# Moving small elementwise work from GpSimd to VectorE and ScalarE, and rotating the dense products over more PSUM banks, in a hybrid diffusion layer

## The chip, the cores and the metric

One core of a Trainium2 chip runs one program with five engines: TensorE (PE in the views, its weight loads PEld), VectorE (DVE), ScalarE (ACT), GpSimd (POOL) and SyncE (SP, which here only issues loads). The metric is device time in microseconds (us) from the program's start to its end, the median of a few executions. The profile is of one further execution.

## The reference, cut to what matters

The layer takes 512 latent tokens and 256 context tokens of width 1024. One wide input projection feeds three parallel branches and their output gates; the branches are merged, projected, and followed by a convolutional feed-forward part.

```
px, pc = split(hx @ w_in), split(hc @ w_in)          # latent, context
# branch a, HGRN2, 4 heads, forward and backward
f = sigmoid-based decay(px[1], lb);  k = (1 - lb) * sigmoid(-px[1])
a = rmsnorm(scan(q, f, k, v), g) * silu(px[4])       # per head, 128 channels
# branch b: grouped attention, 8 heads of 64, keys from context and latent
# branch c, Hyena: u = v * x1; y = irfft(rfft(u) * rfft(kern)) + u * bias; c = y * x0
m = sigmoid(g_a)*(a @ w_oa) + sigmoid(g_b)*(b @ w_ob) + sigmoid(g_c)*(c @ w_oc)
x = x + gate * rmsnorm(m @ w_out)
x = x + gate * rmsnorm((silu(conv(h @ w_up)_1) * conv(h @ w_up)_2) @ w_down)
```

## The kernel before, in words

Activations lie with channels on the partitions and tokens along the free axis. Each float32 operand of a dense product is split into a high and a low part (`split`: ScalarE copies the high part, L204, VectorE subtracts, L207), and a product takes three TensorE passes (`passes`), so that a dense product of 1024 by 128 weights against 512 tokens is 24 matmuls of 512 columns into one PSUM bank.

`Mixer.run` builds a list of such dense jobs: for each head of branch a two gate jobs and one value job, then keys, queries, Hyena inputs, then the merge, the output projection and the feed-forward. `stream` runs the list and loads and splits the weights one job ahead. Beside it run generators for the work that follows from the jobs: `hg_mixes`, `hg_states` and `hg_outputs` for branch a, `hyena` for branch c, `at_prepare`, `all_scores` and `attention` for branch b, and `second` for the norm between the halves. `weave` interleaves them by a planned time: each `yield` of a number is the delay after which a generator's next piece may be emitted. TensorE's order is pinned to that order of emission. The other engines' orders are laid by the framework's scheduler when the program is compiled: it lets a later instruction go ahead where an earlier one is planned to wait. Each engine's queue then runs in the order that was laid.

PSUM has eight banks of 512 float32 columns. `dbank` hands out the banks of `dbanks` in turn to the dense products; `cbank` hands out those of `cbanks` to everything else. Between the first stage and the attention these are two banks and six. A dense product may start when its bank has been read out: by ScalarE and VectorE in `hg_gate` (L638, L639), `conv3` (L888 to L890) or at the merge (L1277, L1292, L1294). The attention sets `dbanks` to [1, 5] while its scores take banks 2 to 4, and at its end to [0, 1]. The first product of the output projection uses bank 0 by name.

The places where GpSimd works before:
- `rstd_` (four calls, one per head of branch a): VectorE adds the epsilon (L872), GpSimd takes the power -0.5 (L873) and then builds four diagonal matrices of 128 by 128 by scaling the identity (L876); TensorE multiplies ones by them to spread the result over the partitions. In the first stage `shares` does the same with the diagonals in one VectorE operation (L470).
- `hg_gate` (16 calls, 8 of 512 columns and 8 of 256): k is the sigmoid times a per-channel factor (L642).
- `hy_spectrum` (two calls): for each of two blocks of frequencies and two signs the complex product of the spectra, of which one of the six operations is on GpSimd (L969) and five on VectorE (L968, L970 to L973); and, once per call, the product for row 0, six operations on one partition (L952 to L957).
- The power of `at_prepare` (L1152) and the load of the transform tables (L340) stay in GpSimd's queue.

Of the kernel before, what the change touches and what calls it, by code (L numbers as in the profile page):

```python
# [15 lines left out]
AF = mybir.ActivationFunctionType  # L16
ALU = mybir.AluOpType
PSUM = bass.MemoryType.PSUM
MUL, ADD, SUB = ALU.mult, ALU.add, ALU.subtract
# [11 lines left out]
C_ID, C_ONE, C_KVB, C_Q2, C_OV, C_WK, C_NWK, C_WKS, C_EPS, C_NH, NCONST = (  # L31
    0, 128, 384, 512, 516, 518, 520, 522, 524, 525, 557)
# [127 lines left out]
class Mixer:  # L160
# [335 lines left out]
    def begin(self):  # L496

        nc, i, v = self.nc, self.i, self.nc.vector
# [98 lines left out]
            pass  # L597
        self.free(cb, m, rows[1], self.slots)
        self.slots = []
        self.dbanks, self.cbanks = [0, 1], [2, 3, 4, 5, 6, 7]  # L600

    def ada_rest(self):

# [28 lines left out]
    def hg_gate(self, ps, n, col, f, k):  # L632

        nc, v = self.nc, self.nc.vector
        s, t = self.A(n), self.A(n)
        s_, t_ = s[:, :n], t[:, :n]
        lo, om = self.lb[:, 16 + col:17 + col], self.lb[:, 24 + col:25 + col]
        nc.scalar.activation(s_, ps, AF.Sigmoid)  # L638
        nc.scalar.activation(t_, ps, AF.Sigmoid, scale=-1.0)  # L639
        v.scalar_tensor_tensor(f, s_, math.exp(30.0), t_, op0=MUL, op1=ALU.min)  # L640
        v.scalar_tensor_tensor(f, f, lo, s_, op0=MUL, op1=ADD)
        nc.gpsimd.tensor_scalar(k, t_, om, 1.0, op0=MUL, op1=MUL)  # L642
        self.free(s, t)

    def group(self, col):
# [217 lines left out]
    def rstd_(self, sqs, ones_col, scale=1.0, n=T, engine=None):  # L863

        nc, v = self.nc, self.nc.vector
        nc_ = n // 128
        ps = self.cbank()
        for j, sq in enumerate(sqs):
            for c in range(nc_):
                self.mm(ps[:, 2 * c:2 * c + 2], sq[:, c * 128:(c + 1) * 128], self.cv(ones_col, 2), j == 0 and c == 0, j == len(sqs) - 1 and c == nc_ - 1)  # L870
        ms = self.A(16)
        v.tensor_scalar(ms[:, 0:nc_], ps.v(0, [(2, nc_)]), scale, EPS, op0=MUL, op1=ADD)  # L872
        nc.gpsimd.tensor_tensor(ms[:, 4:4 + nc_], ms[:, 0:nc_], self.cv(C_NH, nc_), op=ALU.pow)  # L873
        dg = self.A(n)
        for c in range(nc_):
            (engine or nc.gpsimd).tensor_scalar(dg[:, c * 128:(c + 1) * 128], self.cv(C_ID, 128), ms[:, 4 + c:5 + c], 1.0, op0=MUL, op1=MUL)  # L876
        yield 3.5
        rb = self.cbank()
        for c in range(nc_):
            self.mm(rb[:, c * 128:(c + 1) * 128], self.cv(C_ONE, 128), dg[:, c * 128:(c + 1) * 128], True, True)  # L880
        self.free(ms, dg)
        return rb
# [27 lines left out]
    def hy_spectrum(self, ch):  # L910


        nc, v, g = self.nc, self.nc.vector, self.nc.gpsimd
        uT, bufs, Y, K = [], [], {}, self.K
        cs = slice(ch * 256, ch * 256 + 256)
        for par in range(2):
            ps = self.cbank()
            for mc in range(2):
                for ct in range(2):
                    o = (2 * mc + ct) * 128  # L920
                    self.transpose(ps[:, o:o + 128], self.us[2 * ch + ct].v(2 * 128 * mc + par, [(2, 128)]))
            hh, ll = self.R(512), self.R(512)
            self.split(hh.r, ll.r, ps[:])
            uT += [(hh.r[:, mc * 256:mc * 256 + 256], ll.r[:, mc * 256:mc * 256 + 256]) for mc in range(2)]
            bufs += [hh, ll]
        yield 2.5
        for kc in range(2):
            S, y, ks = {}, {}, slice(kc * 256, kc * 256 + 256)
            for half, n in enumerate("cs"):
                ps = self.cbank()  # L930
                pe, po = ps[:, 0:256], ps[:, 256:512]
                self.dft(pe, uT, 2 * half, 0, kc)
                self.dft(po, uT, 2 * half + 1, 1, kc)
                p, e = S[n + "p"], S[n + "m"] = self.A(256), self.A(256)
                nc.scalar.activation(e[:], pe, AF.Copy)
                v.tensor_tensor(p[:], po, e[:], op=ADD)
                if kc == 0:
                    if half == 0:
                        ur = self.A(512)
                    else:  # L940
                        nc.scalar.activation(ur[0:1, :], ps[0:1, :], AF.Copy)
                if half == 0:
                    v.scalar_tensor_tensor(e[:], po, -1.0, e[:], op0=MUL, op1=ADD)
                else:
                    v.tensor_tensor(e[:], po, e[:], op=SUB)
                yield 0.3
            if kc == 0:
                row, t = self.A(512), self.A(256)
                r = row[0:1, :]
                c0, s0 = ur[0:1, 0:256], ur[0:1, 256:512]  # L950
                kc0, ks0 = self.Krow[0:1, cs], self.Krow[0:1, 512 + ch * 256:768 + ch * 256]
                g.tensor_tensor(r[:, 0:256], c0, kc0, op=MUL)  # L952
                g.tensor_tensor(r[:, 256:], c0, ks0, op=MUL)
                g.tensor_tensor(t[0:1, :], s0, ks0, op=MUL)
                g.tensor_tensor(r[:, 0:256], r[:, 0:256], t[0:1, :], op=SUB)
                g.tensor_tensor(t[0:1, :], s0, kc0, op=MUL)
                g.tensor_tensor(r[:, 256:], r[:, 256:], t[0:1, :], op=ADD)  # L957
                self.free(t, ur)
                if ch == 1:
                    self.free(self.Krow)  # L960
            else:
                self.free(bufs)
                if ch == 1:
                    self.free(self.fwd)
            for x in "pm":
                C, Sn, Kc, Ks = S["c" + x], S["s" + x], K["c" + x][ch][:, ks], K["s" + x][ch][:, ks]
                a, b, t = self.A(256), self.A(256), self.A(256)
                v.tensor_tensor(a[:], C[:], Kc, op=MUL)  # L968
                g.tensor_tensor(t[:], Sn[:], Ks, op=MUL)  # L969
                v.tensor_tensor(b[:], C[:], Ks, op=MUL)  # L970
                v.tensor_tensor(a[:], a[:], t[:], op=SUB)
                v.tensor_tensor(t[:], Sn[:], Kc, op=MUL)
                v.tensor_tensor(b[:], b[:], t[:], op=ADD)  # L973
                self.free(t, C, Sn)
                y["c" + x], y["s" + x] = a, b
                yield 2.2
            for n, (a, b, op) in enumerate((("cp", "cm", ADD), ("cp", "cm", SUB), ("sp", "sm", SUB), ("sp", "sm", ADD))):
                t, hl = self.A(256), self.R(512)
                v.tensor_tensor(t[:], y[a][:], y[b][:], op=op)
                if kc == 0 and n >= 2:  # L980
                    v.tensor_copy(t[0:1, :], r[:, (n - 2) * 256:(n - 1) * 256])
                self.split(hl.r[:, 0:256], hl.r[:, 256:512], t[:])
                Y[n, kc] = hl
                self.free(t)
                yield 0.9
            self.free(*y.values())
            if kc == 0:
                self.free(row)
        self.free([k[ch] for k in K.values()])
        return Y  # L990
# [221 lines left out]
    def attention(self):  # L1212
        nc, v = self.nc, self.nc.vector
# [26 lines left out]
        for n in range(16):  # L1240
            yield lambda: n in self.pr
            p, ready = self.pr.pop(n)
            for g in range(3):
                yield max(AT_SPLIT, ready - self.time)
                pt = Buf(self.bank((6, 0)[(n + g) % 2]))
                for j in range(2):
                    for e in range(2):
                        o = (2 * j + e) * 128
                        k = (2 * g + j + 2 * e) % 6 * 128
# [10 lines left out]
        while todo:  # L1260
            yield AT_SPLIT
            values()
        self.dbanks = [0, 1]
        self.free(self.qs, *self.ks[0], *self.ks[1], self.vhl_bufs, self.rq)


# [469 lines left out]
```

## Time and profile before

| what | value |
|---|---|
| median of 3 runs | 1106.04 us (1105.34 to 1109.14) |
| the profiled execution, its own time | 1114.44 us |
| its span, first to last instruction | 1112.7 us |
| mean granted TensorE clock | 0.989 of full speed |
| TensorE busy | 1073.2 us, 96% of the span |
| VectorE busy | 759.3 us, 68% |
| ScalarE busy | 483.3 us, 43% |
| GpSimd busy | 109.4 us, 10% |

Busy time of TensorE counts a matmul from its start to a modelled end, and successive matmuls overlap, so the idle time that is left over is time in which TensorE really had nothing to run. In the timeline rows the first number is the start in us, the second the length of the stretch, and the bracket says how long the engine was idle just before and which engine and line ended that.

### The profile page before, as it was taken

The numbers are of one execution on the slowest core, as the hardware profiler recorded it, in microseconds if no ns is written. First come the engines' busy times: TensorE is split into PE (matmuls) and PEld (weight loads), VectorE is DVE, ScalarE is ACT, GpSimd is POOL, SyncE is SP. The second block draws the span as 40 slices with busy tenths as digits, with TensorE's granted clock in tenths as the row PEclk, the third lists the DMA queues.
The fourth block names the chain that finished last, engine by engine and source line by source line (L and its number), as shares of the span: only waits on it lengthen the run. The fifth ranks groups of instructions, "written<-read, shape, count | busy, mean of one in ns | idle before, by whom it ended". The sixth has DMA issues, their size and how long they took to land.

```text
span 1112.7 us, 14365 instructions
## 1 busy us (share of the span) xinstructions
PE 1073.2 (96%) x5540; PEld 905.2 (81%) x5540; DVE 759.3 (68%) x1262; ACT 483.3 (43%) x751; POOL 109.4 (10%) x130
## 2 busy tenths in 40 slices
PE   8999999999999999999999999989999999999997
PEld 5788888999887787878888877879888888878885
DVE  6999987988876678887666657374686666542223
ACT  3454543343533433855555644274434444322211
POOL 1000202221131203002111100010000000000000
PEclk9999999999998999999999999999999999999999
DMA  9733621251171224231111254120463232222122
GB/s 351 266 108 117 205 96 57 77 189 58 48 233 51 76 76 131 65 108 39 58 57 57 79 171 149 57 64 32 131 216 108 95 113 96 76 76 95 57 95 75
DMA packets 34949, 119.86 MB, mean 108 GB/s; under 512 B 3921, under 2 KB 3921, under 8 KB 34882
## 3 DMA queue, kind: packets, MB, share of 16 engines
q1 hardware_dynamic: 32112, 111.16, 30.2%
q0 software_dynamic: 1392, 4.97, 1.5%
q10 hardware_dynamic: 1378, 2.82, 0.8%
q8 instruction: 43, 0.70, 0.3%
q14 instruction: 24, 0.20, 0.1%
HBM read 116.85 MB, written 2.10 MB: 107 GB/s over the span
## 4 chain that ended last, share of the span: by engine, by line
PE 72%; DVE 10%; issue 7%; ACT 5%; DMA 4%; POOL 3%; SPq 0%; DVEq 0%; POOLq 0%; ACTq 0%
PE banks L249 69%; PE banks L252 2%; DMA page<-in_w_ada 2%; DVE page L207 2%; DVE page L461 1%; ACT page L204 1%; DMA page<-in_xT 1%; DVE page L1094 0%; ACT page L1193 0%; DVE wide L461 0%; DMA w_raw<-in_w_in 0%; DVE page L481 0%; DVE page L1294 0%; POOL page L876 0%; DVE page L807 0%
## 5 line engine op out<-in xcount | busy, mean ns | idle before, releaser
L249 PE MATMUL banks<-hx_h,page 128*128 128x512 f32 (+1 forms) x1776 | 558.8, 385 | 11.0 <-ACT hx_h L482 3.9
L249 PEld LDWEIGHTS banks<-hx_h,page 128*128 128x128 f32 x1776 | 330.8, 190 | 76.5 <-ACT hx_h L482 6.8
L249 PE MATMUL banks<-page,page 128*128 128x512 f32 (+3 forms) x1842 | 359.4, 333 | 6.9 <-ACT page L1193 2.5
L249 PE MATMUL banks<-hx_l,page 128*128 128x512 f32 (+1 forms) x880 | 336.5, 382 | 1.5 <-DVE hx_l L207 1.5
L249 PEld LDWEIGHTS banks<-page,page 128*128 128x128 f32 (+1 forms) x1842 | 283.3, 190 | 50.0 <-issue 6.9
L207 DVE TENSOR_TENSOR page<-w_raw,page 128x1024 fp32r<-128x1024 f32 (+2 forms) x153 | 181.1, 1185 | 165.8 <-ACT page L204 156.3
L204 ACT ACTIVATE page<-w_raw 128x1024 fp32r<-128x1024 f32 (+2 forms) x155 | 158.1, 1022 | 170.6 <-PE banks L249 141.9
L249 PEld LDWEIGHTS banks<-hx_l,page 128*128 128x128 f32 x880 | 167.2, 190 | 30.0 <-DVE hx_l L207 1.7
L249 PE MATMUL banks<-page,thin 128*128 128x512 f32 (+1 forms) x300 | 83.3, 374 | 2.5 <-DVE page L1294 1.7
L461 DVE SCALAR_TENSOR_TENSOR page<-page,page 128x1024 f32<-128x1024 f32 x54 | 65.8, 1221 | 12.7 <-DMA page<-in_w_ada 12.2
L249 PEld LDWEIGHTS banks<-page,thin 128*128 128x128 f32 x300 | 53.8, 190 | 13.3 <-ACT page L204 2.3
L249 PE MATMUL banks<-thin,page 128*128 128x512 f32 (+1 forms) x160 | 47.6, 364 | 1.6 <-ACT thin L204 1.3
L1340 POOL TENSOR_TENSOR page<-page,const 128x1 f32<-128x1 f32 x8 | 4.4, 551 | 449.8 <-DVE page L1339 449.8
L204 ACT ACTIVATE page<-page 128x512 fp32r<-128x512 f32 (+1 forms) x36 | 21.2, 592 | 61.5 <-DVE page L1449 23.5
L1193 ACT ACTIVATE page<-banks,page 128x768 f32<-128x768 f32 x32 | 31.7, 990 | 32.7 <-DVE page L1192 32.6
L1195 POOL TENSOR_SCALAR page<-page,page 128x768 f32<-128x768 f32 x32 | 29.1, 909 | 164.6 <-DVE page L1194 160.7
L252 PE MATMUL banks<-const,page 128*128 128x128 f32 x286 | 42.6, 277 | 1.4 <-ACT page L1418 0.9
L252 PEld LDWEIGHTS banks<-const,page 128*128 128x128 f32 x286 | 35.7, 146 | 9.4 <-ACT page L1418 1.3
L888 ACT ACTIVATE page<-banks,vec 128x512 f32<-128x512 f32 x45 | 34.3, 766 | 10.5 <-PE banks L249 9.6
L791 ACT ACTIVATE page<-wide 128x512 f32<-128x512 f32 x28 | 18.9, 675 | 44.5 <-DVE wide L797 19.2
L889 DVE SCALAR_TENSOR_TENSOR page<-banks,vec,page 128x511 f32<-128x511 f32 x45 | 33.3, 745 | 4.8 <-ACT page L888 4.8
L204 ACT ACTIVATE page<-banks 128x512 fp32r<-128x512 f32 x43 | 25.3, 592 | 24.9 <-PE banks L252 24.9
(279 smaller groups left out, 980.9 us busy)
## 6 DMA issues: line engine op xcount, KB each, us to landing
w_raw<-in_w_in SPq DMA_DIRECT2D x58, 512.0 KB, 3.5
w_raw<-in_w_up SPq DMA_DIRECT2D x44, 512.0 KB, 3.5
page<-in_w_ada SPq DMA_DIRECT2D x43, 512.0 KB, 4.6
w_raw<-in_w_down SPq DMA_DIRECT2D x22, 512.0 KB, 3.5
w_raw<-in_w_out SPq DMA_DIRECT2D x8, 512.0 KB, 4.4
w_raw<-in_w_first SPq DMA_DIRECT2D x8, 384.0 KB, 5.9
wide<-in_w_ada SPq DMA_DIRECT2D x5, 512.0 KB, 7.2
page<-in_fwd POOLq DMA_DIRECT2D x4, 512.0 KB, 5.8
```

Source lines behind the costliest of these rows:

```text
L204: self.nc.scalar.activation(h, x, AF.Copy, scale=1.0 if scale is None else scale)
L207: e.tensor_tensor(l, x, hf, op=SUB)
L249: self.on_pe(self.nc.tensor.matmul(out, w, x, start=start, stop=stop), max(n, 64) * (1 if x.dtype == F32R else 4))
L252: self.on_pe(self.nc.tensor.transpose(out, x, self.cv(C_ID, 128)), 256)
L461: self.nc.vector.scalar_tensor_tensor(junk, w, 1.0, row, op0=MUL, op1=MUL, accum_out=out)
L791: nc.scalar.activation(km.v(0, [(2 * b, n2), (b, 2), (1, b)]), kq.v(1024, [(2 * b, n2), (b - 1024, 2), (1, b)]), AF.Copy)
L888: nc.scalar.activation(out, ps, AF.Identity, bias=w[:, 3:4], scale=w[:, 1:2])
L889: v.scalar_tensor_tensor(out[:, 1:T], ps[:, 0:T - 1], w[:, 0:1], out[:, 1:T], op0=MUL, op1=ADD)
L1193: nc.scalar.activation(p[:], s, AF.Exp, bias=st[:, 1:2], scale=r, accum_out=st[:, 2:3])
L1195: gp.tensor_scalar(p[:], p[:], st[:, 3:4], 1.0, op0=MUL, op1=MUL)
L1340: nc.gpsimd.tensor_tensor(q, q, self.cv(C_NH), op=ALU.pow)
```

## The change

The four diagonals of `rstd_` become one VectorE operation with a broadcast of the identity and of the four columns. The product for k in `hg_gate` becomes a ScalarE copy with a per-channel scale. All of `hy_spectrum`'s GpSimd operations move to VectorE, the six of row 0 (one is shown) and L969. From the end of the first stage the dense products rotate over three banks instead of two, and the rest over five instead of six; at the merge after the attention the dense products rotate over four.

```diff
-        self.dbanks, self.cbanks = [0, 1], [2, 3, 4, 5, 6, 7]
+        self.dbanks, self.cbanks = [0, 1, 2], [3, 4, 5, 6, 7]
...
-        nc.gpsimd.tensor_scalar(k, t_, om, 1.0, op0=MUL, op1=MUL)
+        nc.scalar.activation(k, t_, AF.Copy, scale=om)
...
-        for c in range(nc_):
-            (engine or nc.gpsimd).tensor_scalar(dg[:, c * 128:(c + 1) * 128], self.cv(C_ID, 128), ms[:, 4 + c:5 + c], 1.0, op0=MUL, op1=MUL)
+        v.tensor_tensor(dg.v(0, [(128, nc_), (1, 128)]), Buf(self.const).v(C_ID, [(0, nc_), (1, 128)]), ms.v(4, [(1, nc_), (0, 128)]), op=MUL)
...
-                g.tensor_tensor(r[:, 0:256], c0, kc0, op=MUL)
+                v.tensor_tensor(r[:, 0:256], c0, kc0, op=MUL)
...
-                g.tensor_tensor(t[:], Sn[:], Ks, op=MUL)
+                v.tensor_tensor(t[:], Sn[:], Ks, op=MUL)
...
-        self.dbanks = [0, 1]
+        self.dbanks = [0, 1, 2, 3]
```

## Rows read from the trace of the kernel before

**Rows 1.** The page: span, and busy time of each engine.
```profile
span 1112.7 us, 14365 instructions
PE 1073.2 (96%) x5540; PEld 905.2 (81%) x5540; DVE 759.3 (68%) x1262; ACT 483.3 (43%) x751; POOL 109.4 (10%) x130
```

**Rows 2.** Windows by stage: length, busy per engine, granted clock, DMA share, GB/s.
```profile
56.00:112.00 56.00, 56.00 (x254) 46.50 (x253) 54.09 (x109) 29.15 (x40) 1.62 (x1) 1.00 0.36 114
112.00:327.00 215.00, 210.81 (x1367) 188.80 (x1366) 183.56 (x331) 89.54 (x152) 38.23 (x45) 1.00 0.36 113
...
346.00:448.00 102.00, 97.03 (x471) 81.23 (x470) 77.27 (x153) 40.73 (x69) 18.89 (x24) 0.98 0.28 91
...
645.00:740.00 95.00, 86.68 (x397) 70.05 (x395) 55.77 (x86) 46.07 (x81) 5.76 (x7) 0.97 0.34 111
740.00:1092.00 352.00, 350.87 (x1677) 295.54 (x1676) 182.17 (x228) 129.09 (x171) 0.77 (x2) 1.00 0.30 96
```

**Rows 3.** Timeline of TensorE, the stretches that begin with a wait.
```profile
126.71 0.50 PE L249 MATMUL banks<-hx_h,page 128*128 128x512 f32 x1 [0.75 <-ACT page L639]
...
333.06 0.49 PE L249 MATMUL banks<-page,const 128*128 128x128 f32 x2 [1.62 <-POOL page L876]
...
335.55 0.80 PE L249 MATMUL banks<-page,const 128*128 128x128 f32 x2 [0.88 <-POOL page L876]
336.00 0.77 PE L249 MATMUL banks<-hx_h,page 128*128 128x512 f32 x1
...
389.35 0.77 PE L249 MATMUL banks<-hx_h,page 128*128 128x512 f32 x1 [2.69 <-DVE page L890]
...
427.52 0.51 PE L249 MATMUL banks<-hx_h,page 128*128 128x512 f32 x1 [2.28 <-DVE page L1292]
...
472.89 3.01 PE L249 MATMUL banks<-page,page 128*128 128x512 f32 x12 [0.66 <-ACT page L1277]
...
684.45 0.94 PE L249 MATMUL banks<-page,thin 128*128 128x512 f32 x3 [1.67 <-DVE page L1294]
```

**Rows 4.** Windows around two of these waits (columns as in rows 2).
```profile
334.50:344.70 10.20, 9.32 (x29) 7.60 (x28) 4.13 (x9) 1.26 (x2) 3.55 (x2) 0.51 0.19 69
...
389.10:392.50 3.40, 3.15 (x8) 2.51 (x9) 3.37 (x10) 0.88 (x3) 0.00 (x0) 0.53 0.00 0
392.50:395.90 3.40, 3.40 (x16) 2.81 (x15) 3.12 (x9) 1.63 (x3) 0.00 (x0) 0.97 0.41 134
```

**Rows 5.** Timeline of GpSimd.
```profile
238.57 2.02 POOL L873 TENSOR_TENSOR page<-page,const 128x4 f32<-128x4 f32 x1
...
331.40 1.09 POOL L873 TENSOR_TENSOR page<-page,const 128x4 f32<-128x4 f32 x1
332.59 2.91 POOL L876 TENSOR_SCALAR page<-const,page 128x128 f32<-128x128 f32 x4
...
387.03 0.71 POOL L957 TENSOR_TENSOR page<-page,page 1x256 f32<-1x256 f32 x1
```

**Rows 6.** Timeline of VectorE.
```profile
387.78 0.43 DVE L970 TENSOR_TENSOR page<-page,thin 128x256 f32<-128x256 f32 x1 [3.64 <-POOL page L957]
...
421.60 0.94 DVE L968 TENSOR_TENSOR thin<-page,thin 128x256 f32<-128x256 f32 x1 [1.16 <-POOL thin L953]
...
683.02 0.69 DVE L207 TENSOR_TENSOR page<-w_raw,thin 128x512 fp32r<-128x512 f32 x1
683.62 0.68 DVE L1294 SCALAR_TENSOR_TENSOR page<-page,banks 128x512 f32<-128x512 f32 x1
```

**Rows 7.** Groups by line and form, VectorE: busy, mean ns, idle before, releaser.
```profile
L968 DVE TENSOR_TENSOR page<-page,thin 128x256 f32<-128x256 f32 x6 | 2.5, 413 | 0.0
...
L470 DVE TENSOR_TENSOR page<-const,page 128x512 f32<-128x512 f32 x1 | 0.7, 693 | 0.9 <-POOL page L469 0.9
```

**Rows 8.** Groups by line and form, ScalarE (columns as in rows 7).
```profile
L791 ACT ACTIVATE page<-wide 128x512 f32<-128x512 f32 x28 | 18.9, 675 | 44.5 <-DVE wide L797 19.2 <-PE banks L249 12.2 <-DVE page L641 11.9
...
L204 ACT ACTIVATE page<-page 128x256 fp32r<-128x256 f32 x6 | 2.5, 419 | 14.4 <-DVE page L979 12.9 <-DVE page L981 1.6
```

**Rows 9.** Who waited for whom, TensorE alone: total us, times, longest.
```profile
PE banks L249 <- POOL page L876: 3.3, 4, 1.6
...
PE banks L249 <- DVE page L790: 1.3, 3, 0.6
```

More of the change, by code (lines that the diff above doesn't have):

```diff
@@ L910, in hy_spectrum @@
     def hy_spectrum(self, ch):
-        nc, v, g = self.nc, self.nc.vector, self.nc.gpsimd
+        nc, v = self.nc, self.nc.vector
         uT, bufs, Y, K = [], [], {}, self.K
@@ L951, in hy_spectrum @@
                 kc0, ks0 = self.Krow[0:1, cs], self.Krow[0:1, 512 + ch * 256:768 + ch * 256]
-                g.tensor_tensor(r[:, 0:256], c0, kc0, op=MUL)
[L953 to L957, printed above, removed]
+                v.tensor_tensor(r[:, 0:256], c0, kc0, op=MUL)
+                v.tensor_tensor(r[:, 256:], c0, ks0, op=MUL)
+                v.tensor_tensor(t[0:1, :], s0, ks0, op=MUL)
+                v.tensor_tensor(r[:, 0:256], r[:, 0:256], t[0:1, :], op=SUB)
+                v.tensor_tensor(t[0:1, :], s0, kc0, op=MUL)
+                v.tensor_tensor(r[:, 256:], r[:, 256:], t[0:1, :], op=ADD)
                 self.free(t, ur)
```

## The prediction, made before the changed kernel ran

> **What bounds the kernel now.** I read the page first. TensorE is busy 1073.2 of 1112.7 us, every other engine far less [rows 1], so the time is TensorE's work plus the places where it stands or runs at a lower clock; a change that adds and removes nothing on TensorE can only win or lose there. The windows by stage say where that is. From 740 us on it is 350.87 of 352 busy: nothing this early change saves is likely to be soaked up there, and it has nothing to win there either. The stages that the edits touch, 112 to 448 and 645 to 740, leave some 4, 5 and 8 us idle, with VectorE at 183.56 of 215 us (85%) in the first of them [rows 2]. Next I read TensorE's timeline for the stretches that begin with a wait and the releaser named in each [rows 3]; then the granted clock behind the longer of these waits [rows 4]; then GpSimd's and VectorE's timelines, for what the releaser had itself waited for [rows 5, 6].
>
> Four kinds of wait belong to the edits:
> - The fourth head's diagonals: TensorE idles 1.62 and 0.88 us between small matmuls that each need one more diagonal, and dense work resumes at 336.00 [rows 3]. GpSimd takes 2.91 us for the four [rows 5].
> - The spectra: at 389.35 a dense product waits 2.69 us for L890 to read out its bank [rows 3]; VectorE was held 3.64 us before L970 by GpSimd's row products, which end with L957 [rows 5, 6]. At 427.52 it is 2.28 us for L1292, in the second call of the same code [rows 3].
> - Banks read out a little late: 0.75 us at 126.71 (L639) and 0.66 at 472.89 (L1277) [rows 3].
> - The merge's end: 1.67 us at 684.45 for L1294 [rows 3]. Counting `dbank` calls, 10 in the first stage, 36 up to the merge, 48 in it, the last is number 94: over two banks it falls on bank 0, which the output projection's first tile uses by name.
>
> After two of these waits the clock is lower: 0.51 over 334.5 to 344.7, and 0.53 over 389.1 to 392.5, which is the lower level, 1.2 GHz instead of 2.4; 8 matmuls ran there, and 16 in the next 3.4 us [rows 4].
>
> **The change, part by part.** *Spectra.* GpSimd's 8 L969 and 12 row products become VectorE operations. A 128x256 product takes VectorE 0.413 us [rows 7]; a 1x256 product has no row on VectorE, and I bound it by 0 and the same 0.413, taking the upper end, the nearest row with as many columns. That is 20 x 0.413 = 8.3 us more on VectorE, in a stage where it has 102 - 77.27 = 24.7 us free [rows 2], and half a call's share (8 operations before L890, 3.3 us) replaces the 3.64 us it stood idle. So L890 comes hardly later, and a third bank gives the waiting product one more dense group, 24 matmuls, before it needs that bank. I take both waits as gone: 2.69 + 2.28 = 4.97 us, and with the first the slow stretch, where half of 3.4 us was lost: 1.7. Bounds: with the bank alone freed but the next weight split then late, none; all of it, 6.7.
>
> *Three banks.* The waits at 126.71 and 472.89 are for banks whose successor would now be a third: 0.75 + 0.66 = 1.4 us, between 0 and that. The other work's banks fall from six to five; rows 3 and 9 show no TensorE wait for such a bank that a sixth had averted, so 0, with 1 us as the other bound (the size of the waits seen).
>
> *Diagonals.* Four operations of GpSimd become one of VectorE of the form of L470, 0.693 us [rows 7]. At the fourth head the power ends at 331.40 + 1.09 = 332.5 [rows 5]. If VectorE is free at once the diagonals are ready at 333.2, if it first does a weight split of 1.2 us (two L207 halves of 0.69 less overlap) [rows 6], at 334.4; the eight short passes take about 1 us, so dense work resumes between 334.2 and 335.4 instead of 336.00. I take 1.2 us of gain, bounds 0.6 and 1.8. The wait that remains, some 2 us, may still lower the clock; but the second gap is gone, so I take one slow stretch like that at 389.1 rather than 10.2 us: half of 10.2 - 3.4 = 3.4, discounted to 3.0; bounds 0 and 5.1. At the three other heads a new wait appears: the diagonals stand in VectorE's queue behind a power that takes 1.09 to 2.02 us [rows 5], and the level copies L790 to L797 are queued behind them; TensorE waits for L790 already (1.3 us, three times) [rows 9]. `shares` shows the same pair: VectorE stood only 0.9 us, since the scheduler filled in other work [rows 7]. Per head the delay is 0.69 at least and 2.02 + 0.69 = 2.7 at most for VectorE; what reaches TensorE lies between 0 and that. I take 0.5 each: 1.5 us of loss.
>
> *k on ScalarE.* Eight copies at 0.675 and eight at 0.419 [rows 8]: 8.8 us more, in a stage where ScalarE is busy 89.54 of 215 [rows 2]. They stand behind the sigmoids that read out the bank, so they delay no read-out but what is next in the queue: level copies (L791) or the high parts of weights (L204). Cover: ScalarE's idle time before L791, 44.5 us [rows 8]. I take 0.5 us of loss; without the cover 8.8.
>
> Sharing between VectorE and GpSimd: L968 took 0.94 us while GpSimd ran a row product, 0.413 otherwise [rows 6, 7]. The change ends most such meetings; I put nothing for it into the sum. The Trainium skill, "SBUF — State Buffer", section "Who interferes with whom", says that a VectorE instruction with two SBUF inputs contends with a GpSimd instruction that reads SBUF, the later one waiting. By that rule each of the 14 L642 of 112 to 327 could free up to half a microsecond of VectorE time there, an estimate of at most 7 us of VectorE time, none of it TensorE's directly. The trace agrees where the two overlap.
>
> *Four banks at the merge.* Over four banks product 94 falls on bank 94 mod 4 = 2, and bank 0 holds number 92, read out two products earlier. But the weights' low part (L207 at 683.02, 0.69 long) was itself only just ahead of L1294 [rows 6], so the second matmul would wait until about 683.7 against 684.3: gain 0.6, bounds 0 and 1.67.
>
> **The sum.** Gains 5.0 + 1.7 + 1.4 + 1.2 + 3.0 + 0.6 = 12.9; losses 1.5 + 0.5 = 2.0, and 0.3 for scores that may find bank 2 not yet read out (one case in three, about 1 us like the late banks above). Net 10.6 us. The profiled execution took 1114.44 us, 1.74 around its span of 1112.7, and 8.4 more than the median of the runs, 1106.04; I carry the difference over unchanged: 1106.0 - 10.6 = 1095.4.
>
> **Rivals.**
> 1. *The slow stretch stays and the diagonals win nothing* (1099 to 1102). The fourth head's wait begins where VectorE and GpSimd's own L1152 delay the power; the diagonals are a part of it only. Then 1.2 + 3.0 fall away: 1099.6. For it: the wait that remains is close to those after which the clock fell. Chance 0.17.
> 2. *The waits move to the next supply* (1103 to 1109). A product that starts earlier finds its weights not split. For it: VectorE is 85% busy, and at 683 the split is 0.6 us behind the bank. Against it: the spectra's waits are VectorE's own idle time. Then the bank waits (5.0 + 1.4 + 0.6) and the clock behind them (1.7) are not won, and 10.6 - 8.7 = 1.9 us is left: 1104. Chance 0.12.
> 3. *All of it and more* (1084 to 1090): upper bounds 6.7 + 1.4 + 1.8 + 5.1 + 1.67 + 1.3 from L790 give 18: 1088. Chance 0.11.
> 4. *Slower: VectorE's queue held behind the power.* Between L872 and its diagonal VectorE can stand for GpSimd's whole chain: about 1.2 us at two heads and 3 us at the two where a table load or L1152 goes ahead of L873, plus 4 x 0.69: 11.2 us. If all of it passes to TensorE through L790, and three of the four stops are followed by a slow stretch of 1.7 us, that is 16.3 us against 12.9 - 3.0 won elsewhere: 1112. It decides once more than 13 us of VectorE's delay reaches TensorE. Against it: TensorE's waits for L790 sum to 1.3 us though VectorE is 85% busy. Chance 0.08.
> 5. *More banks make the clock oscillate.* If every change of bank cost a slow stretch, forty dense products at 1.7 us would cost up to 68 us. Against it: the stages with five and four banks, 56 to 112 and 740 to 1092, ran at 1.00 [rows 2]. The Trainium skill, "TensorE: Matmul & The Clock Gate", section "A second HAM failure mode: psum-queue depth-cycling", describes a kernel whose clock went up and down as it cycled through banks. The traces bear it out nowhere here. Chance 0.02.
>
> **How the numbers follow.** My forecast, 1090 to 1099, has 0.50. Differences under 0.3%, 3.3 us, can't be told from none. Faster is forecast, rivals 1 and 3: 0.78. Of rival 2 its range straddles the border; nearly all is within it: 0.12. Slower are rivals 4 and 5: 0.10. The range from 1087 to 1104 holds the forecast, rival 1, three quarters of rival 3 and a quarter of rival 2, 0.78; its ends are the upper bounds and a gain of 2 us.
>
> **What the changed profile would show.** Right: no VectorE idle before L970 for GpSimd; no TensorE wait near 389 and 427, and no slow stretch at 389; one VectorE operation of 0.69 us for the diagonals, dense work resuming about 1 us after it; GpSimd busy some 45 us less; the wait at the merge's end under 1.1 us. Wrong: TensorE waits for L790 adding up to over 3 us, VectorE idle of 2 us or more before the diagonals at every head, waits for L207 where the bank waits were, or new slow stretches elsewhere, since a new wait of some 2 us can cost as much as it lasts again.

## The result, and the profile of the changed kernel

The changed kernel takes 1095.04 us, median of 4 runs (1094.32 to 1095.99); the kernel before took 1106.99 in the runs beside it. The ratio is 0.988, with a 95% interval of 0.9854 to 0.9906: faster, by 10.4 to 16.2 us of 1107. The forecast was 1095.4. (Ratios here and below are of the timed runs of one comparison and differ a little from the quotient of the medians.)

The page of the changed kernel, the lines that answer to [rows 1]:

```profile
span 1093.4 us, 14321 instructions
PE 1064.7 (97%) x5540; PEld 900.8 (82%) x5540; DVE 759.4 (69%) x1286; ACT 492.0 (45%) x767; POOL 62.2 (6%) x78
```

TensorE runs the same 5540 matmuls, GpSimd is busy 47.2 us less, ScalarE 8.7 us more. VectorE has 24 more instructions and is no busier, which the last section comes back to.

The windows by stage, changed kernel (columns as in rows 2; the last two are the two stretches in which the clock was low):

```profile
112.00:327.00 215.00, 212.49 (x1381) 191.17 (x1380) 185.11 (x342) 99.57 (x170) 12.02 (x18) 1.00 0.37 118
...
346.00:448.00 102.00, 102.00 (x548) 88.05 (x548) 86.37 (x183) 49.46 (x85) 2.17 (x4) 1.00 0.29 93
448.00:500.00 52.00, 48.17 (x231) 39.40 (x230) 39.40 (x65) 31.73 (x51) 6.74 (x8) 0.97 0.22 72
478.10:481.50 3.40, 3.40 (x13) 2.91 (x14) 1.22 (x3) 0.07 (x1) 0.91 (x1) 0.54 0.00 0
...
717.00:720.40 3.40, 3.26 (x15) 3.26 (x16) 1.20 (x3) 2.27 (x4) 1.10 (x1) 0.54 0.78 265
```

The stage of the spectra is full: 102.00 of 102 us against 97.03 [rows 2], at a clock of 1.00. The attention's start, 448 to 500, is not: 3.8 us stand idle there, and a slow stretch lies in it.

TensorE's timeline, changed kernel: the places of [rows 3], and the longest wait of this stage.

```profile
329.12 1.16 PE L249 MATMUL banks<-page,const 128*128 128x128 f32 x8 [0.17 <-DVE page L875]
330.04 0.47 PE L249 MATMUL banks<-hx_h,page 128*128 128x512 f32 x1
...
381.12 1.60 PE L249 MATMUL banks<-page,page 128*128 128x256 f32 x12
...
410.38 0.39 PE L249 MATMUL banks<-hx_h,page 128*128 128x512 f32 x1
...
477.94 0.90 PE L249 MATMUL banks<-page,page 128*128 128x256 f32 x4 [3.26 <-ACT page L1192]
...
665.60 0.84 PE L249 MATMUL banks<-page,thin 128*128 128x512 f32 x3
```

The eight small matmuls of the fourth head now run in one piece. The products that had waited for the spectra have no bracket any more, nor has the first product of the output projection at 665.60. (A line was removed from the code, so lines after 876 count one less: L1192 is the exponential that was L1193, L875 the diagonals.)

The profile of before was of an execution of 1114.44 us, and the accounts below need one nearer to the median. A second execution of the unchanged kernel took 1106.34 us, with a span of 1104.5 and a clock of 0.996. Its TensorE timeline at the same places:

```profile
330.51 1.18 PE L249 MATMUL banks<-page,const 128*128 128x128 f32 x6 [0.29 <-POOL page L876]
331.45 0.48 PE L249 MATMUL banks<-hx_h,page 128*128 128x512 f32 x1
...
380.68 0.47 PE L249 MATMUL banks<-hx_h,page 128*128 128x512 f32 x1 [2.70 <-DVE page L890]
...
387.15 1.12 PE L249 MATMUL banks<-page,page 128*128 128x256 f32 x8
...
418.84 0.73 PE L249 MATMUL banks<-hx_h,page 128*128 128x512 f32 x1 [2.27 <-DVE page L1292]
...
488.02 0.74 PE L249 MATMUL banks<-page,page 128*128 128x256 f32 x4 [1.81 <-ACT page L1193]
...
676.36 0.93 PE L249 MATMUL banks<-page,thin 128*128 128x512 f32 x3 [1.66 <-DVE page L1294]
```

And its windows, at the fourth head (where the first execution had its long slow stretch) and behind the two spectra waits:

```profile
334.50:344.70 10.20, 10.20 (x46) 8.42 (x45) 9.09 (x15) 5.24 (x8) 2.55 (x1) 1.00 0.12 42
...
381.10:384.50 3.40, 3.40 (x11) 2.62 (x10) 3.37 (x9) 1.55 (x3) 0.00 (x0) 0.54 0.00 0
418.70:422.10 3.40, 3.26 (x8) 2.62 (x9) 3.40 (x8) 1.14 (x2) 0.00 (x0) 0.53 0.21 69
```

Read side by side, the two timelines say where the time came from. Each line is the start of the same matmul:

| place | before, second execution | changed | earlier by |
|---|---|---|---|
| dense work after the fourth head's diagonals | 331.45 | 330.04 | 1.4 |
| behind the first spectrum's slow stretch | 387.15 | 381.12 | 6.0 |
| the product that waited for L1292 | 418.84 | 410.38 | 8.5 |
| the second attention block's scores | 488.02 | 477.94 | 10.1 |
| first product of the output projection | 676.36 | 665.60 | 10.8 |
| the span | 1104.5 | 1093.4 | 11.1 |

The spectra give most of it: 4.6 us at the first (its wait of 2.70 and 1.7, half of the 3.4 us at half the clock, make 4.4 of it), 2.5 at the second before its slow stretch counts, and 1.7 more by that stretch. At the attention's start 3.1 us are given back: a wait of 3.26 instead of 1.81, and 1.7 for the slow stretch at 478.1.

### The profile page after: what moved, and what is told of

It is laid out like the page before. It is cut to its first block, busy times and chain, and to the rows that moved or that the text cites. A ratio compares the mean times of both kernels' runs of the same rounds, so it can differ in the third digit from the quotient of the medians.

```text
span 1093.4 us, 14321 instructions
## 1 busy us (share of the span) xinstructions
PE 1064.7 (97%) x5540; PEld 900.8 (82%) x5540; DVE 759.4 (69%) x1286; ACT 492.0 (45%) x767; POOL 62.2 (6%) x78
## 4 chain that ended last, share of the span: by engine, by line
PE 75%; DVE 10%; ACT 6%; DMA 4%; issue 3%; POOL 1%; SPq 0%; DVEq 0%; ACTq 0%; POOLq 0%
PE banks L249 73%; DMA page<-in_w_ada 2%; PE banks L252 2%; DVE page L207 2%; ACT page L204 2%; DVE page L461 2%; DMA page<-in_xT 1%; DMA w_raw<-in_w_in 1%; ACT thin L1076 1%; ACT page L1192 1%; ACT page L1076 0%; ACT page L1392 0%; DVE wide L461 0%; POOL page L1391 0%; DMA w_raw<-in_w_up 0%
## 5 line engine op out<-in xcount | busy, mean ns | idle before, releaser
L207 DVE TENSOR_TENSOR page<-w_raw,page 128x1024 fp32r<-128x1024 f32 (+2 forms) x153 | 180.7, 1183 | 160.5 <-ACT page L204 153.3
L204 ACT ACTIVATE page<-w_raw 128x1024 fp32r<-128x1024 f32 (+2 forms) x155 | 158.1, 1022 | 167.8 <-PE banks L249 138.9
L461 DVE SCALAR_TENSOR_TENSOR page<-page,page 128x1024 f32<-128x1024 f32 x54 | 65.8, 1221 | 11.0 <-DMA page<-in_w_ada 10.9
L249 PEld LDWEIGHTS banks<-page,thin 128*128 128x128 f32 x300 | 53.3, 189 | 11.1 <-DVE page L207 1.1
L1192 ACT ACTIVATE page<-banks,page 128x768 f32<-128x768 f32 x32 | 31.7, 991 | 31.3 <-DVE page L1191 29.1
L204 ACT ACTIVATE page<-page 128x512 fp32r<-128x512 f32 (+1 forms) x36 | 21.3, 593 | 50.8 <-DVE page L1448 24.2
L887 ACT ACTIVATE page<-banks,vec 128x512 f32<-128x512 f32 x45 | 34.3, 767 | 10.1 <-PE banks L249 8.9
L204 ACT ACTIVATE page<-banks 128x512 fp32r<-128x512 f32 x43 | 25.3, 593 | 27.5 <-PE banks L252 27.4
L249 PEld LDWEIGHTS banks<-thin,page 128*128 128x128 f32 x160 | 29.4, 194 | 5.9 <-ACT thin L204 1.8
```

Of the source, the lines that this page charges most:

```text
L204: self.nc.scalar.activation(h, x, AF.Copy, scale=1.0 if scale is None else scale)
L207: e.tensor_tensor(l, x, hf, op=SUB)
L249: self.on_pe(self.nc.tensor.matmul(out, w, x, start=start, stop=stop), max(n, 64) * (1 if x.dtype == F32R else 4))
L461: self.nc.vector.scalar_tensor_tensor(junk, w, 1.0, row, op0=MUL, op1=MUL, accum_out=out)
L887: nc.scalar.activation(out, ps, AF.Identity, bias=w[:, 3:4], scale=w[:, 1:2])
L1192: nc.scalar.activation(p[:], s, AF.Exp, bias=st[:, 1:2], scale=r, accum_out=st[:, 2:3])
```

## The experiments

A diff is against the kernel before where the text says "alone", otherwise against the changed kernel.

**The banks alone.** The edit is the two lines of the banks, nothing else.

```diff
-        self.dbanks, self.cbanks = [0, 1], [2, 3, 4, 5, 6, 7]
+        self.dbanks, self.cbanks = [0, 1, 2], [3, 4, 5, 6, 7]
...
-        self.dbanks = [0, 1]
+        self.dbanks = [0, 1, 2, 3]
```

> The kernel before with the bank rotations alone (three and five, four at the merge); GpSimd keeps all its work. Theory 1, the waits near 389 and 427 us were for a bank, and a third bank is cushion enough though VectorE still stands for GpSimd: both waits gone (5.0 us) with the slow stretch (1.7), late banks (1.4) and the merge's end (1.7) too; the fourth head's diagonals stay. So some 8 to 10 us off, less 1 to 3 us that comes back as a longer wait at the attention's start: 1098 to 1101 us, VectorE's 3.6 us idle before L970 still there. Theory 2, the next product's weight split is queued behind the same stop of VectorE, so a bank alone only moves the wait: waits of 2 us or more on TensorE at the same places, now ended by L207, and 1103 to 1106 us.

Measured: 1105.55 us against 1107.32, ratio 0.9968 (0.9938 to 0.9998). TensorE's timeline of this kernel, its new waits:

```profile
405.05 0.39 PE L249 MATMUL banks<-page,page 128*128 128x256 f32 x1 [2.14 <-ACT page L204]
405.77 1.09 PE L249 MATMUL banks<-page,page 128*128 128x256 f32 x6 [0.34 <-DVE page L207]
...
487.82 0.77 PE L249 MATMUL banks<-page,page 128*128 128x256 f32 x4 [3.80 <-ACT page L1193]
```

VectorE's timeline of the same kernel, and a window behind the first of these waits:

```profile
380.42 0.43 DVE L970 TENSOR_TENSOR page<-page,thin 128x256 f32<-128x256 f32 x1 [3.66 <-POOL page L957]
```

```profile
406.20:409.60 3.40, 3.40 (x16) 3.11 (x15) 0.97 (x3) 0.38 (x1) 0.00 (x0) 0.54 0.00 0
```

The third bank takes away the long bank waits, as meant (two short ones for L1277 are left, 0.54 us at 465.49 and 0.88 at 481.69). But VectorE still stands 3.66 us for GpSimd's row, its chain ends no earlier, and TensorE now waits 2.14 + 0.34 us for the split of the second spectrum's input (L204, L207), with a slow stretch behind it, and 2 us longer at the attention. The wait moved, as the second theory has it. This is rival 2's mechanism, with another releaser than the weight split that I had named.

**The engines alone**: all the moves to VectorE and ScalarE, the banks as before (the two lines above undone in the changed kernel).

> The changed kernel with the bank rotations of before (two and six, two at the merge). Theory 1: the spectra's waits are gone, since VectorE no longer stands, and the diagonals' too; the small bank waits stay (0.75 and 0.66 us, 1.67 at the merge's end). 1097 to 1100 us. Theory 2 (VectorE's stop is the whole cause, the banks add nothing): the same as the changed kernel within 1 us, 1094 to 1096. If instead the products put on VectorE delay its read-outs as much as its waiting did, waits of 2 us near 389 and 427 stay and it is 1103 or more.

Measured: 1098.64 us, ratio 0.9897 (0.9859 to 0.9935). TensorE's timeline of this kernel:

```profile
127.69 0.50 PE L249 MATMUL banks<-hx_h,page 128*128 128x512 f32 x1 [0.87 <-ACT page L639]
...
411.20 0.50 PE L249 MATMUL banks<-hx_h,page 128*128 128x512 f32 x1 [0.80 <-DVE page L1291]
...
456.95 3.01 PE L249 MATMUL banks<-page,page 128*128 128x512 f32 x12 [1.07 <-ACT page L1276]
...
479.29 0.74 PE L249 MATMUL banks<-page,page 128*128 128x256 f32 x4 [1.80 <-ACT page L1192]
```

The long spectra waits are gone without any bank; short ones stay, the three shown for a bank and 1.4 us for L1293 at the merge's end, 4.1 us in all. In medians the banks add 3.6 us to the engines (1098.64 to 1095.04) and 1.8 by themselves. The intervals overlap, so that the banks win more once VectorE's chain is no longer behind them is what the rows suggest, not what the times show.

**The spectra alone**: of the changes only the seven lines of `hy_spectrum`.

```diff
-                g.tensor_tensor(r[:, 0:256], c0, kc0, op=MUL)
+                v.tensor_tensor(r[:, 0:256], c0, kc0, op=MUL)
...
-                g.tensor_tensor(t[:], Sn[:], Ks, op=MUL)
+                v.tensor_tensor(t[:], Sn[:], Ks, op=MUL)
```

> The kernel before with one part of the change alone: the spectra's products on VectorE; diagonals, k and banks as before. Theory 1, this part is the core of the gain: both waits of 2.3 to 2.9 us and what the clock lost after each are gone, 4.2 to 4.5 us apiece, some of it given back at the attention's start: 1098 to 1101 us against 1106 to 1107, no VectorE idle for GpSimd's row products. Theory 2, VectorE only has room for these products once k and the diagonals have left GpSimd, or once a third bank cushions them: a wait of 1.5 us or more stays at either place, 1102 to 1105.

Measured: 1100.13 us against 1107.5, ratio 0.9944 (0.992 to 0.9967), which is 3.7 to 8.9 us. My two terms for the spectra, 5.0 + 1.7, lie inside, and the time is in the range of the first theory.

**Without the spectra**: the changed kernel with these lines back on GpSimd.

> The changed kernel with the spectra's products on GpSimd again, as before. Theory 1, the third bank is cushion enough: within 1.5 us of the changed kernel (1094 to 1097), no TensorE wait over 1 us near the spectra, VectorE idle some 3.6 us before L970. Theory 2: waits of 2 us or more there, ended by a weight split or a read-out, 1099 to 1103.

Measured: 1101.07 us, ratio 0.9944 (0.9923 to 0.9965), 6.0 us above the changed kernel's median. TensorE waits 2.18 + 0.34 us for L204 and L207 at 402.49 and 403.22, the wait of the banks alone. The third bank is no cushion for it: the second theory.

**The diagonals alone.**

```diff
-        for c in range(nc_):
-            (engine or nc.gpsimd).tensor_scalar(dg[:, c * 128:(c + 1) * 128], self.cv(C_ID, 128), ms[:, 4 + c:5 + c], 1.0, op0=MUL, op1=MUL)
+        v.tensor_tensor(dg.v(0, [(128, nc_), (1, 128)]), Buf(self.const).v(C_ID, [(0, nc_), (1, 128)]), ms.v(4, [(1, nc_), (0, 128)]), op=MUL)
```

> The kernel before with the diagonals on VectorE as the one edit. If my sum's terms for them hold (1.2 us at the fourth head, 3.0 us of clock behind it, 1.5 us lost at the other heads), the median is 2.7 us below that of the kernel before, ratio 0.9976. If the 10.2 us slow stretch at the fourth head belonged to the one execution profiled and not to the kernel, the diagonals are worth 0.7 to 0.8 us of wait and no clock: ratio 0.9993, within the 0.3% that can't be told from no change. If VectorE's queue is held behind the power at every head (up to 13 us of its time), the median is above the kernel before and TensorE's waits for L790 add up to over 3 us. The profile's two spectra waits (2.2 to 2.9 us, for L890 and L1291) should be there unchanged in every case.

Measured: 1104.44 us against 1106.71, ratio 0.9978 (0.996 to 0.9996), 0.4 to 4.4 us. Both sizes that were to be told apart, 2.7 and 0.7 to 0.8, lie in this interval; "no gain at all" does not. TensorE's timeline of this kernel, and a window behind the first spectrum's wait:

```profile
330.51 1.16 PE L249 MATMUL banks<-page,const 128*128 128x128 f32 x8
...
380.80 0.47 PE L249 MATMUL banks<-hx_h,page 128*128 128x512 f32 x1 [2.70 <-DVE page L889]
...
418.05 0.50 PE L249 MATMUL banks<-hx_h,page 128*128 128x512 f32 x1 [2.28 <-DVE page L1291]
```

```profile
383.40:386.80 3.40, 3.40 (x21) 3.01 (x20) 3.12 (x9) 2.01 (x4) 0.00 (x0) 1.00 0.31 87
```

The fourth head has no wait at all. Of the two spectra waits, as long as in the unchanged kernel, neither was followed by a slow stretch in this execution.

**Without the diagonals**: the changed kernel with the four operations back on GpSimd.

> The changed kernel with the four diagonals of each head on GpSimd again. Theory 1, the fourth head's wait with what the clock lost after it is worth 4 to 7 us: 1098 to 1102 us, and TensorE waits for the diagonals at the fourth head for 2.5 us or more, with the lower clock behind it. Rival, the diagonals were only in the way because VectorE and GpSimd disturbed each other, and with k and the spectra gone from GpSimd they come in time: 1094 to 1096.

Measured: 1096.85 us, ratio 0.9899 (0.9852 to 0.9947), with the changed kernel's span, 1093.4. TensorE's waits for L876 there sum to 0.4 us, and no slow stretch lies behind them. The time lies between the two ranges; the waits are those of the rival, the diagonals come in time. What the diagonals give is too small to be seen beside the rest.

**The unchanged kernel again**, no edit, for a second profile.

> The kernel before, unchanged, for a second profile. If the 10.2 us slow stretch at the fourth head belongs to the kernel, it is there again, and the span is 1110 to 1114 us. If it belongs to that one execution (how the waits fell that time), the stretch is absent or 3.4 us long and the span some 3 to 6 us shorter, with the waits of 2.7 us near 389 and 2.3 near 427 still there.

It is the execution shown above. What made the first one's fourth head late is seen in part on VectorE, at L461, where the modulation's weights are used; first the kernel before in the first execution, then in the second:

```profile
327.63 1.23 DVE L461 SCALAR_TENSOR_TENSOR page<-page,page 128x1024 f32<-128x1024 f32 x1 [1.13 <-DMA page<-in_w_ada]
```

```profile
324.39 1.22 DVE L461 SCALAR_TENSOR_TENSOR page<-page,page 128x1024 f32<-128x1024 f32 x1 [0.20 <-DMA page<-in_w_ada]
```

VectorE stood 0.9 us longer for a load of the modulation's weights, and queued behind it on VectorE were the read-out L851 and the epsilons L1151 and L872 that GpSimd's powers wait for. GpSimd's diagonals then took 2.91 us [rows 5] instead of 1.89; why is not shown. TensorE's waits were 1.62 + 0.29 + 0.88 us in one execution and 0.29 in the other. Two more kernels leave `rstd_` as before, the spectra alone and the banks alone. TensorE's timeline, in this order:

```profile
332.39 1.18 PE L249 MATMUL banks<-page,const 128*128 128x128 f32 x6 [0.29 <-POOL page L876]
```

```profile
331.46 1.53 PE L249 MATMUL banks<-page,const 128*128 128x128 f32 x8 [1.47 <-POOL page L876]
```

With these and the changed kernel without the diagonals, GpSimd made them in five profiled executions. The wait was 0.3 to 0.5 us in three, 1.47 in one and 2.79 in one, and only behind the last was the clock low.

**k on GpSimd**, the rest as changed.

```diff
-        nc.scalar.activation(k, t_, AF.Copy, scale=om)
+        nc.gpsimd.tensor_scalar(k, t_, om, 1.0, op0=MUL, op1=MUL)
```

> The changed kernel with the product for k on GpSimd again (16 of L642's operations). My sum put 0.5 us of loss on ScalarE for it, so without that move the time should be within 1 us of the changed kernel: 1094 to 1096 us. Rival: GpSimd's products lengthen VectorE's operations beside them, and the level copies or the fourth head come late: TensorE's waits for L790 over 1 us in all, 1097 to 1100.

Measured: 1097.42 us, ratio 0.9914 (0.9887 to 0.9941). That is 2.4 us above the changed kernel in medians, in another comparison and with overlapping intervals; the spans differ by 0.7. The time is in the rival's range, but TensorE's waits for L790 are 0.7 us in all, not over 1. No loss by ScalarE shows; whether there is a gain stays open.

**The merge over two banks**, the rest as changed (`self.dbanks = [0, 1]` at the attention's end).

> The changed kernel with two banks at the merge, as before. The wait at the merge's end comes back: 1.5 to 1.7 us on L1294's line. My sum had put only 0.6 us on it, because the weights' low part was to be late instead: 1095.5 to 1096 by the sum, 1096.5 to 1097.5 if the whole wait counts.

Measured: 1096.39 us, ratio 0.9898 (0.9874 to 0.9923). TensorE's timeline of this kernel:

```profile
664.71 0.93 PE L249 MATMUL banks<-page,thin 128*128 128x512 f32 x3 [1.58 <-DVE page L1293]
```

The whole wait is back: four banks are worth 1.6 us here, by this row alone. The times can't show it; the profiled execution's span, 1092.6 us, is even below the changed kernel's.

**The attention's start.** Three kernels try to win back the 3.1 us given back there, by moving the order of emission: the transposes of the first block's probabilities 3.5 us later, or the second block's scores 3.4 or 5 us later.

```diff
-            self.pr[n] = self.scores(n // 2, n % 2), self.time + AT_PROB
+            self.pr[n] = self.scores(n // 2, n % 2), self.time + AT_PROB + (3.5 if n == 0 else 0.0)
```

> The changed kernel with the first attention block's transposes planned 3.5 us later, so that dense matmuls stand there instead of a 3.3 us wait for the first exponentials with a slow stretch behind it. If that wait is really lost time, 3 to 5 us less: 1090 to 1092 us, no wait over 1 us at the attention's start and no slow stretch there. If the later start only moves it (the second block or the attention's end then wait for it), 1094 to 1096.

```diff
-            yield AT_EXP
+            yield AT_EXP + (3.4 if n == 0 else 0.0)
```

> The changed kernel with the second attention block's scores planned 3.4 us later, so that TensorE runs dense work and the first block's transposes before them. Theory: the 3.3 us wait at the attention's start, with the slow stretch behind it, stands before those scores, whose banks the first block's exponentials still read; 3 to 5 us less than the changed kernel, 1090 to 1092. Rival: the first block's transposes wait for the same exponentials, so the wait stays within 1 us of its length: 1094 to 1096.

> The same with 5.0 us in place of 3.4. Theory: no wait over 0.5 us is left at the attention's start and the time is that of the 3.4 us version within 1 us, 1090 to 1092; if the later scores starve the softmax instead, a new wait of 1 us or more comes with the third block and it is 1093 or more.

Measured: 1094.29 us, ratio 0.9883 (0.9863 to 0.9903), for the first; 1096.91, 0.9906 (0.9882 to 0.993), and 1095.01, 0.9895 (0.9874 to 0.9915), for the others. The first still waits 3.78 us for L1192. TensorE's timeline of the second:

```profile
477.65 0.90 PE L252 MATMUL banks<-const,page 128*128 128x128 f32 x3 [2.55 <-POOL page L1194]
...
489.89 0.74 PE L249 MATMUL banks<-page,page 128*128 128x256 f32 x4 [1.77 <-ACT page L1192]
```

With the scores out of the way TensorE waits 2.55 us for the same chain's next link, GpSimd's scaling of the probabilities, and the 5 us version 2.56 for the same. That points to the chain and not the order as the limit; no version can be told from the changed kernel.

## Why the prediction was right, and which of its terms were not

The time came out 0.4 us from the forecast, and that it came so near is luck: some terms of the sum were wrong and offset each other. What was right is the mechanism of the spectra, and that neither rival 2 nor rival 4 would eat up the gain. Each term is held against the second execution of the unchanged kernel:

| term | forecast | shown |
|---|---|---|
| two spectra waits | +5.0 | +5.0 (2.70 + 2.27 gone) |
| clock behind them | +1.7 | +3.4 in this execution (two stretches of 3.4 us; one in the first profile) |
| late banks at 127 and 473 | +1.4 | +1.4 (0.8 and 0.6 in its list of waits, both gone) |
| fourth head's wait | +1.2 | +0.6 (below) |
| clock behind it | +3.0 | 0 |
| merge's end | +0.6 | +1.7 (1.66 gone) |
| L790 behind the diagonals | -1.5 | +0.6 |
| k on ScalarE, bank 2 | -0.8 | no loss seen |
| attention's start | not in the sum | -3.1 (1.45 of wait, 1.7 of clock) |

*The spectra* went as worked out. VectorE's timeline, changed kernel, around the read-out that had been late:

```profile
372.42 0.40 DVE L951 TENSOR_TENSOR page<-page,page 1x256 f32<-1x256 f32 x1
...
375.43 0.40 DVE L956 TENSOR_TENSOR page<-page,page 1x256 f32<-1x256 f32 x1
375.76 0.73 DVE L889 SCALAR_TENSOR_TENSOR page<-banks,vec,page 128x511 f32<-128x511 f32 x1
...
666.10 0.68 DVE L207 TENSOR_TENSOR page<-w_raw,thin 128x512 fp32r<-128x512 f32 x1
```

The product on one partition takes 0.40 us, the upper end that I took, and VectorE goes straight on to the read-out L889. The runs with one part alone show that the engines carry this and that the banks alone would have ended in rival 2. The clock's 3.4 is this execution's: with the diagonals alone the same two waits cost none of it.

*The fourth head's terms, 1.2 + 3.0, were the step that failed.* I read the long wait and the 10.2 us stretch as the kernel's. They were that execution's, one of five: a late load, and slower diagonals after it. I had also carried the profiled execution's 8.4 us above the median over unchanged; the terms that I took from that surplus could not be won from the median. The mechanism was right: VectorE makes the diagonals at once in 0.69 us, and dense work resumes 0.9 us after the first small matmul (329.12 to 330.04), where the second execution before took 1.7 (from 329.74, two matmuls ahead of the stretch shown, to 331.45); less the wait of 0.17 that is 0.6. That the diagonals alone win 0.4 to 4.4 us leaves room for executions of either kind.

*The losses of the diagonals* did not come. TensorE's waits, changed kernel (total us, times, longest):

```profile
PE banks L249 <- ACT page L1192: 3.8, 3, 3.3
...
PE banks L249 <- DVE page L875: 0.6, 2, 0.5
PE banks L249 <- DVE page L790: 0.4, 1, 0.4
```

L790 is waited for once, 0.4 us, against 1.0 in three waits in the second execution before and 1.3 in the first [rows 9]. VectorE stands 4.5 us in all ahead of the four diagonals, about 1.1 each, and this shows on TensorE only at their own matmuls (0.45 us at 240.32, 0.17 at the fourth head): rival 4's price was right in kind and far from the 13 us from which it decides.

*The merge's end* was under-sized. I held the low part at L207 for the next limit. In the changed kernel VectorE writes it from 666.10 on, half a microsecond after TensorE has begun the product at 665.60 without a wait; the first matmuls do not need it. So the whole wait was the bank's.

*The attention's start* was the unforeseen term, and it comes with the banks. "Nothing is likely to be soaked up" was said of the time from 740 us on, and there it held. Here the wait before the second block's scores is 1.76 to 1.81 us in all five profiles with two banks, though with the engines alone they start 8.7 us earlier (479.29 against 488.02); the chain that they wait for, on VectorE and ScalarE, had moved along with TensorE. With three banks it is 3.26 us in the changed kernel and 3.80 with the banks alone. Against the engines alone TensorE comes to these scores 2.8 us earlier in the changed kernel, and they start 1.35 us earlier (477.94): half of what the banks had won by then stayed. Whether the third bank does it or the one bank fewer for the other work, no run parts. That the chain does not come earlier because of VectorE's queue in front of it was argued from the timeline; no run took that queue away.

Rival 5 is refuted for these bank counts: the clock was 0.995 in the mean, and its two low stretches between the first and the last microseconds stand behind waits (3.26 us at 477.94; 1.24 and 1.51 us at 715.25 and 717.14), not behind changes of bank. The oscillation that the Trainium skill describes under "TensorE: Matmul & The Clock Gate", section "A second HAM failure mode: psum-queue depth-cycling", is in no run here.

The terms as shown add up to 9.6 us (5.0 + 3.4 + 1.4 + 0.6 + 1.7 + 0.6 - 3.1) of the 11.1 between the spans, but the table is not complete. The changed kernel's first dense product starts 0.9 us later (24.07 against 23.13), it lost the 0.45 us at 240.32 and some 1.7 us by the clock at 717, which the second execution did not lose, and its waits for L1392 are 1.4 us shorter. That leaves some 3 us of smaller differences that are not attributed.

## What to carry to other kernels

A long wait in one profile is worth asking whether a load released it: if so it may be that execution's and not the kernel's, and a second profile of the unchanged kernel is the cheapest way to find out before a price is put on it. A buffer and the engine that empties it are two edits of one wait: freeing the buffer alone moved the wait to the next consumer of the same chain, while moving the spectra's work alone won some 7 us. And whoever comes earlier by a freed buffer arrives earlier at the next chain that did not move along: look for that meeting point, and count what is given back there.

## What the hardware showed that I had not expected

*The clock after equal waits.* Waits of 2.70 and 2.27 us at the spectra were followed by 0.54 and 0.53 of the clock in one execution of the unchanged kernel; of the 2.69 and 2.28 in the first, only the former was [rows 3, 4]; in the kernel with the diagonals alone, 2.70 and 2.28 us, neither was. The wait of 1.80 us at 479.29 with the engines alone was followed by a slow stretch, the 1.81 at 488.02 in the unchanged kernel was not. And two waits in a row, 1.24 and 1.51 us, were followed by 0.54 at 717 in the changed kernel; the same two in the second execution of the unchanged one, 1.24 us at 726.08 and 1.50 at 727.97, were followed by 1.00. TensorE's timeline, first the changed kernel (its window is shown above), then the other, with its window:

```profile
717.14 0.48 PE L249 MATMUL banks<-hx_l,page 128*128 128x256 f32 x1 [1.51 <-DVE hx_l L207]
```

```profile
727.97 0.38 PE L249 MATMUL banks<-hx_l,page 128*128 128x256 f32 x1 [1.50 <-DVE hx_l L207]
```

```profile
727.90:731.30 3.40, 2.71 (x21) 2.51 (x22) 1.20 (x3) 2.34 (x4) 1.02 (x1) 1.00 0.78 254
```

What tells these cases apart no run here shows, so a term for the clock behind a wait of this size is a chance and not a price.

*VectorE's work for nothing.* It took over 20 products and 4 diagonals, 20 x 0.41 + 4 x 0.69 = 11.0 us by their rows, and its busy time went from 759.3 to 759.4. Others became shorter, by 8 us in all, 3.8 of it the spectra's other products and 2.3 those of `hg_gate`; the rest of the 11.0 is where successive operations overlap, which these rows count in full. VectorE's groups, first in the kernel before, then in the changed one, then the page of the changed kernel with k on GpSimd:

```profile
L641 DVE SCALAR_TENSOR_TENSOR page<-page,page,page 128x512 f32<-128x512 f32 x8 | 7.4, 924 | 0.1
```

```profile
L641 DVE SCALAR_TENSOR_TENSOR page<-page,page,page 128x512 f32<-128x512 f32 x8 | 6.0, 748 | 0.1
```

```profile
PE 1065.0 (97%) x5540; PEld 900.6 (82%) x5540; DVE 762.8 (70%) x1286; ACT 483.4 (44%) x751; POOL 82.5 (8%) x94
```

With k alone back on GpSimd VectorE is 3.4 us busier. I had put nothing for this into the sum. The Trainium skill's rule on VectorE and GpSimd ("SBUF — State Buffer", section "Who interferes with whom") fits it, and my estimate by it, at most 7 us for k (I had counted 14 of the 16 operations), was twice what showed.
